# Passages between the layers of a seven-product feed-forward: the sixth product's epilogue first, the seventh's parted, its casts behind a bank copy

## The chip, the cores and the metric

The kernel runs on one core of a Trainium2 chip. The metric is the device time of one execution in microseconds (us); lower is better. Before the change the median of three runs is 3420.51 us (3419.1 to 3424.62). One further execution was taken with the profiler; all rows of the trace come from that one.

The engines are TensorE (PE in the profile; PEld is its load of weights), VectorE (DVE), ScalarE (ACT), GpSimd (POOL) and SyncE (SP, which issues the loads from memory). Each works through its own instructions in order and waits at an instruction until what it needs is there.

## The reference

Two blocks run on 512 tokens of width 1024. The first has a hybrid mixer (gated delta rule and retention) and a feed-forward; the second has two layers, each with a feed-forward, a second mixer and another feed-forward. The change lies in the feed-forward alone, of which there are five:

```
def swiglu(h, w_in, w_out):
    gate, up = jnp.split(h @ w_in, 2, axis=-1)
    return (jax.nn.silu(gate) * up) @ w_out
# first block:  D_FF = 2816, x + g2 * swiglu(modulate(rms_norm(x)))
# second block: D_FF_2 = 2816, layer_norm(ALPHA * x + 0.5 * swiglu(x)), twice in each of 2 layers
```

Everything is in float32. The products run on TensorE as three products of halves: every operand is cast to a rounded high part and a rest, and high·high + high·rest + rest·high is summed.

## The kernel before, in words

**Quads and seven products.** In a feed-forward, `run_quads` takes most of the matrix work. A `Quad` is a 2 by 2 arrangement of weight blocks that meets a 2 by 2 arrangement of activations (`Left`, with the slots A11, A12, A22 and the sums S1 to S4). Instead of eight block products it needs seven, called `mm(e,j)` with j from 1 to 7. Each takes 6·nk matmuls of 128x256, where nk is 4 for quads of the first layer (w1, reading the tile `xa`) and 3 or 2 for quads of the second (w2, reading the tile `hl`, the hidden values). A product accumulates in PSUM: products 1 and 2 in a tile `pj`, product 4 in another, products 3, 5, 6 and 7 in one of three banks `sd`.

**Epilogues.** After product j stands `after(e,j)`: after 1 ScalarE copies the PSUM tile to a bank (`L177`), after 3 and 5 it copies banks on (`L179`, `L181`), after 2, 5, 6 and 7 the use of the quad follows. For a quad of the first layer the use is `gated`: after 6 (`c12`) VectorE forms half of the hidden block h (L257, L259), and `c12b` splits it into the slots A11 and A12 of `hl` (ScalarE's cast L80, VectorE's rest L81). After 7 (`c21`) ScalarE takes the Silu (L264) and VectorE forms the other half (L265); `c21b` and `c21c` form the sums (L113 to L120) and split S2, A22 and S3 into `hl`.

**Weights.** Each product's weights are cast by ScalarE (L164, `cast`) and the rest is formed by VectorE (L166, `rest`); sums of weight blocks are VectorE's L161. The products are cast two positions ahead; three places for cast weights go round (two pairs `whi`/`wlo` and one inside the tile `xa`).

**Groups and passages.** The eleven hidden blocks of a feed-forward are worked in the groups (0,3), (3,3), (6,2), (8,3), the first two blocks by plain products. In each of the first three groups the quads of w1 are followed by two quads of w2, called O1 and O2 here, which read what the group has just written to `hl`. The last w1 quad of the group is called L. So there are three passages to a feed-forward, from L to O1 and O2, and 15 in all. The order of products there is (L,2) ... (L,6), (L,7), (O1,1), (O2,1), (O1,2), (O1,3) ... (O1,6), (O1,7), (O2,2) and so on; then the next w1 quad N begins. O1 and O2 have nk = 3 in the first two groups and nk = 2 in the third. (O1,1) reads A11 and (O1,2) reads A12 of `hl`; (O1,3) reads S2; (O1,7) reads A22. (O1,2) accumulates onto (O1,1) in the same PSUM tile, so it must come after the copy L177 has read that tile.

**Order of the work.** `run_quads` writes the order out by hand for PE, ACT, DVE and SP. At position s it first issues the loads, then the matmuls of product s, then the epilogue of product s-1, the sums of weights, one waiting step of other quads (`step`), and the cast and rest of product s+2. At a passage, while `late` holds, the sums and the cast and rest come ahead of the epilogue: in the kernel before, `late` holds for products 6 and 7 of L. L has a use of its own, `at_once`, which does everything after product 7 in one step.

Of the kernel before, what the change touches and what calls it, by code (L numbers as in the profile page):

```python
# [73 lines left out]
def tmp(e,n=512,name="t"):  # L74
    return e.tp.tile([P,512],F32,tag="t",name=name,bufs=e.tb)

def pair(t): return t.rearrange("p (a b) -> p a b",a=2)
# [112 lines left out]
def run_quads(e, quads, extra):  # L190

    ET=mybir.EngineType
    seq=[]; left=None; done=set()
    for i,q in enumerate(quads):
        if q.needs and left: seq.append((left,7)); left=None
        if q not in done: seq.append((q,1))
        if q.needs: seq.append((quads[i+1],1)); done.add(quads[i+1])
        if left: seq.append((left,7))  # L200
        seq+=[(q,j) for j in (2,3,4,5,6)]; left=q
    seq.append((left,7))
    pos={(id(q),j):s for s,(q,j) in enumerate(seq)}
    at={}; free=-99
    for q in quads:
        g=lambda j: pos[id(q),j]
        for s,t in ((g(1)-6,0),(g(3)-9,5),(g(2)-8,6),(max(g(3)-6,free),3),(g(3)-4,1),(g(3)-3,2),(g(5),4)): at.setdefault(s,[]).append((q,t))
        free=g(5)-1
    with e.tc.manual_schedule(engines={ET.PE,ET.Activation,ET.DVE,ET.SP}):
        for s in range(min(at),len(seq)+1):  # L210
            for q,t in at.get(s,[]):
                if t in (0,5,6): q.load(e,t)
            put=None; keep=None
            if s>0: put=seq[s-1]
            if 0<=s<len(seq):
                q,j=seq[s]
                for d in q.needs:
                    if j==1: d.all(6)
                    if j==3: d.all(7)
                if j==2 and put==(q,1): q.after(e,1); put=None  # L220
                q.mm(e,j)
                if j==7 and s+1<len(seq) and seq[s+1][1]==2: keep=seq[s+1][0]
            nx=seq[s+2] if 0<=s+2<len(seq) else None
            late=put and put[1] in (6,7) and any(put[0] is q.needs[-1] for q in quads if q.needs)
            def weights():
                for q,t in at.get(s,[]):
                    if t in (1,2,3,4): q.sum(e,t)
                if nx and late: nx[0].cast(e,nx[1]); nx[0].rest(e,nx[1])
            if late: weights()
            if put and not (put[1]==1 and put[0] in done): put[0].after(e,put[1])  # L230
            if not late: weights()
            for q in quads:
                for j in (2,5,6,7):
                    if s>0 and (q,j)!=put: q.step(j)
            if keep in done: keep.after(e,1)
            for f in extra.get(s,[]): f()
            if nx and not late: nx[0].cast(e,nx[1]); nx[0].rest(e,nx[1])
        for q in quads:
            for j in (2,5,6,7): q.all(j)
# [3 lines left out]
def htile(e): return e.fp.tile([P,4,256],F32,tag="h",name="h",bufs=3)  # L243
# [7 lines left out]
def gated(e, H, i, hscale, sums, last):  # L251

    nc=e.nc; u=Use()
    def c11(ps):
        u.g=e.ea.tile([P,512],F32,tag="ea",name="g0",bufs=2); nc.scalar.activation(u.g,ps,AF.Silu)
    def c12(ps,E):
        t=tmp(e); nc.vector.tensor_add(t,ps,E)  # L257
        u.h=htile(e)
        nc.vector.scalar_tensor_tensor(u.h[:,0:2,:],pair(u.g),hscale,pair(t),op0=ALU.mult,op1=ALU.mult)  # L259
    def c12b(ps,E): H.first(e,i,u.h[:,0:2,:])  # L260
    def c22(ps,E):
        u.t=tmp(e); nc.vector.tensor_sub(u.t,E,ps)
    def c21(ps):
        g=tmp(e); nc.scalar.activation(g,ps,AF.Silu)  # L264
        nc.vector.scalar_tensor_tensor(u.h[:,2:4,:],pair(g),hscale,pair(u.t),op0=ALU.mult,op1=ALU.mult)  # L265
    v=nc.vector
    def part(p): u.s=H.sums(e,i,u.h[:,0:2,:],u.h[:,2:4,:],p,v,p and u.s); return u.s
    def c21b(ps):
        if sums: u.p0=part(0); u.p1=part(1)
        if last: H.puts(e,i,0,u.p0)  # L270
        H.second(e,i,u.h[:,2:4,:])
        if last: H.puts(e,i,1,u.p1)
    def c21c(ps):
        if sums and not last: H.puts(e,i,0,u.p0); H.puts(e,i,1,u.p1)
    u.c11,u.c12,u.c22,u.c21=[c11],[c12,c12b],[c22],[c21,c21b,c21c]
    if last:
        def at_once(ps): c21(ps); c21b(ps)
        u.c21=[at_once]
    return u

GAB=4
# [3 lines left out]
def ffn(e, w1, w2, acc, hscale, ln):  # L285

    nc=e.nc
    with ExitStack() as cf:
# [30 lines left out]
        for g,(j0,n) in enumerate(GROUPS):  # L319
            last=g==len(GROUPS)-1  # L320
            G=[Quad(e.XA,w1[j],4,gated(e,HP if last else H,j-j0,hscale,not last,not last and j==j0+n-1)) for j in range(max(j0,PLAIN),j0+n)]; Q+=G
            if not last: Q+=[out_quad(e,H,w2[g][i],n,4*i,lambda m,sl,ps,sgn,new,g=g: acc(g,m,2,sl,pair(ps),sgn,new),() if i else G) for i in range(2)]
            else:
                x={2: [lambda: hsums(PLAIN-1)]}
                run_quads(e,Q,x)
                stage2(e,[w2[g][m//4][m%4] for m in range(8)],2*n,lambda m,sl,ps: acc(g,m,1,sl,ps,1,True),ln,HP)
# [1062 lines left out]
```

## Time and profile before

| what | value |
|---|---|
| median of three runs | 3420.51 us |
| profiled execution, its own time | 3430.6 us |
| its span, first to last instruction | 3428.8 us |
| TensorE busy | 3263.1 us, 95% of the span |
| TensorE weight load busy | 2989.2 us, 87% |
| VectorE busy | 2539.7 us, 74% |
| ScalarE busy | 1709.2 us, 50% |
| mean granted TensorE clock | 0.98 of full speed |

The profiled execution's own time is 1.8 us more than its span and 10.1 us more than the median of the runs. A row of a wait names who waited, for whom, the total, how often, and the longest. A row of the timeline gives the start, the length, engine, line, operation, output and inputs, how many instructions are merged in it, and in brackets how long the engine stood idle before it and who released it. Matmuls follow each other at a shorter distance than the length of one, so the start of the next row tells more than the length.

### The profile page before, as it was taken

How to read it: one execution, taken by the hardware profiler on the slowest of the kernel's cores; microseconds unless marked ns; L12 is line 12 of the kernel's file. 1: busy time of each engine (PE TensorE's matmuls, PEld its weight loads, DVE VectorE, ACT ScalarE, POOL GpSimd, SP SyncE). 2: the span in 40 equal slices, each digit the busy share in tenths (PEclk: the TensorE clock that was granted, in tenths of full speed). 3: DMA queues.
4: the chain of work that ended last, by engine and by line, in shares of the span. 5: the costliest groups of instructions: out<-in, count | busy, mean ns of one | idle time of the engine just before them, and what ended most of it. 6: DMA issues, size and time to landing. Idle time of an engine off the chain costs nothing. (4 is left out here: it accounts for less than half of the span.)

```text
span 3428.8 us, 54643 instructions
## 1 busy us (share of the span) xinstructions
PE 3263.1 (95%) x22011; PEld 2989.2 (87%) x22011; DVE 2539.7 (74%) x4101; ACT 1709.2 (50%) x2640; POOL 199.3 (6%) x237
## 2 busy tenths in 40 slices
PE   6989889899999999999999999999999999999998
PEld 3767778899999999878889999999998788899998
DVE  5858877789968988653447888788976634368987
ACT  4544544455555555672224555545546822245554
POOL 3241221000000000110000000000000100000000
PEclk9999999999999999999999999999999999999999
DMA  6221214222332323333331233322332233322232
GB/s 207 67 70 44 74 57 141 82 97 96 100 114 74 105 99 99 99 93 97 95 116 52 91 102 104 102 71 93 99 107 97 94 97 99 98 83 85 93 105 62
DMA packets 103502, 322.09 MB, mean 94 GB/s; under 512 B 11472, under 2 KB 15184, under 8 KB 103248
## 3 DMA queue, kind: packets, MB, share of 16 engines
q1 hardware_dynamic: 102464, 316.04, 28.8%
q8 instruction: 173, 2.83, 0.3%
q0 software_dynamic: 640, 2.10, 0.2%
q14 instruction: 81, 0.66, 0.1%
q10 hardware_dynamic: 144, 0.45, 0.0%
HBM read 316.45 MB, written 2.10 MB: 93 GB/s over the span
## 5 line engine op out<-in xcount | busy, mean ns | idle before, releaser
L43 ACT CAST xa<-wraw 128x1024 fp32r<-128x1024 f32 (+1 forms) x200 | 202.4, 1016 | 385.2 <-PE pj L71 150.0
L166 DVE TENSOR_TENSOR wlo<-wraw,whi 128x1024 fp32r<-128x1024 f32 (+2 forms) x295 | 316.3, 1074 | 48.3 <-ACT whi L164 46.1
L70 PE MATMUL pj<-xa 128*128 128x512 f32 (+1 forms) x968 | 343.1, 355 | 1.4 <-ACT X L966 1.4
L72 PE MATMUL pj<-xa 128*128 128x512 f32 (+1 forms) x968 | 341.9, 354 | 0.0
L71 PE MATMUL pj<-xa 128*128 128x512 f32 (+1 forms) x968 | 341.3, 353 | 0.0
L44 DVE TENSOR_TENSOR xa<-wraw,xa 128x1024 fp32r<-128x1024 f32 (+1 forms) x190 | 224.5, 1184 | 110.0 <-ACT xa L43 108.1
L164 ACT CAST whi<-wraw 128x1024 fp32r<-128x1024 f32 (+2 forms) x295 | 272.3, 926 | 61.5 <-DVE wraw L161 26.2
L129 PE MATMUL sd<-xa,whi 128*128 128x256 f32 x1760 | 229.1, 283 | 0.0
L129 PEld LDWEIGHTS sd<-xa,whi 128*128 128x128 f32 x1760 | 219.1, 192 | 0.0
L129 PE MATMUL sd<-xa 128*128 128x256 f32 x1680 | 213.0, 283 | 0.0
L129 PEld LDWEIGHTS sd<-xa 128*128 128x128 f32 x1680 | 206.6, 192 | 0.0
L70 PEld LDWEIGHTS pj<-xa 128*128 128x128 f32 x968 | 187.1, 193 | 21.9 <-ACT X L966 1.8
L71 PE MATMUL sd<-xa 128*128 128x512 f32 (+1 forms) x600 | 204.7, 341 | 0.0
L70 PE MATMUL sd<-xa 128*128 128x512 f32 (+1 forms) x600 | 203.8, 341 | 0.9 <-DVE X L1230 0.9
L129 PE MATMUL pj<-xa,whi 128*128 128x256 f32 x1520 | 200.0, 285 | 4.2 <-ACT sd L177 4.2
L71 PEld LDWEIGHTS pj<-xa 128*128 128x128 f32 x968 | 187.2, 193 | 19.2
L72 PE MATMUL sd<-xa 128*128 128x512 f32 (+1 forms) x600 | 203.8, 340 | 0.0
L72 PEld LDWEIGHTS pj<-xa 128*128 128x128 f32 x968 | 186.9, 193 | 18.7
L129 PEld LDWEIGHTS pj<-xa,whi 128*128 128x128 f32 x1520 | 190.9, 193 | 5.9 <-ACT sd L177 5.5
L44 DVE TENSOR_TENSOR wlo<-wraw,whi 128x1024 fp32r<-128x1024 f32 (+1 forms) x88 | 109.1, 1241 | 97.6 <-ACT whi L43 97.1
L166 DVE TENSOR_TENSOR xa<-wraw,xa 128x1024 fp32r<-128x1024 f32 (+2 forms) x155 | 169.5, 1094 | 16.0 <-ACT xa L164 14.4
L43 ACT CAST whi<-wraw 128x1024 fp32r<-128x1024 f32 (+1 forms) x88 | 90.1, 1025 | 183.1 <-issue 93.2
(560 smaller groups left out, 8235.2 us busy)
## 6 DMA issues: line engine op xcount, KB each, us to landing
wraw<-in_f_dram SPq DMA_DIRECT2D x176, 512.0 KB, 4.0
wraw<-in_win_dram SPq DMA_DIRECT2D x144, 512.0 KB, 3.5
wraw<-in_f_dram SPq DMA_DIRECT2D x96, 384.0 KB, 3.2
wraw<-in_ff_dram SPq DMA_DIRECT2D x44, 512.0 KB, 4.0
raw<-in_ada_dram SPq DMA_DIRECT2D x48, 256.0 KB, 2.6
wraw<-in_ff_dram SPq DMA_DIRECT2D x24, 384.0 KB, 3.2
wraw<-in_ada_dram SPq DMA_DIRECT2D x16, 512.0 KB, 3.9
wraw<-in_f_dram SPq DMA_DIRECT2D x32, 256.0 KB, 2.8
```

The lines of the kernel that those rows point to most:

```text
L43: nc.scalar.copy(hi[:,:n],raw[:,:n])
L44: (nc.gpsimd if e.wi%e.gp==0 else nc.vector).tensor_sub(lo[:,:n],raw[:,:n],hi[:,:n].bitcast(F32))
L70: nc.tensor.matmul(o,lhsT=hi[:,c],rhs=ah,start=start and k==k0,stop=False)
L71: nc.tensor.matmul(o,lhsT=hi[:,c],rhs=al,start=False,stop=False)
L72: nc.tensor.matmul(o,lhsT=lo[:,c],rhs=ah,start=False,stop=stop and k==nk-1)
L129: nc.tensor.matmul(ps[:,p*256:p*256+256],lhsT=w[:,j:j+128],rhs=A.t[:,c,k,l,:],start=first,stop=last,skip_group_check=True)
L164: s.w[j]=hilo_tile(e); e.nc.scalar.copy(s.w[j][0][:,:s.n],s.raw(j)[:,:s.n])
L166: hi,lo=s.w[j]; n=s.n; e.nc.vector.tensor_sub(lo[:,:n],s.raw(j)[:,:n],hi[:,:n].bitcast(F32))
```

## The change

Three things change in `run_quads` and `gated`, all at the 15 passages. `late` holds for product 7 of L only: after product 6 the epilogue `c12` comes ahead of the sum of weights and of the cast and rest of (O2,1), and the split of A11 and A12 (`all(6)`) follows in the same step, ahead of that cast too. L's epilogue after product 7 is parted: `c21s` takes the Silu, the second half of h and the sums, and `c21p` does the three splits. `c21p` is called one position later, by `all(7)`, behind `after(O1,1)`, which is the copy L177 of O1's first bank.

```
-            late=put and put[1] in (6,7) and any(put[0] is q.needs[-1] for q in quads if q.needs)
+            late=put and put[1]==7 and any(put[0] is q.needs[-1] for q in quads if q.needs)
...
             if late: weights()
             if put and not (put[1]==1 and put[0] in done): put[0].after(e,put[1])
             if not late: weights()
+            if s+1<len(seq) and seq[s+1][0].needs and seq[s+1][1]==1: put[0].all(6)
+            if s>1 and seq[s-1][0].needs and seq[s-1][1]==1: seq[s-1][0].needs[-1].all(7)
...
     def c21b(ps):
         if sums: u.p0=part(0); u.p1=part(1)
-        if last: H.puts(e,i,0,u.p0)
         H.second(e,i,u.h[:,2:4,:])
-        if last: H.puts(e,i,1,u.p1)
     def c21c(ps):
-        if sums and not last: H.puts(e,i,0,u.p0); H.puts(e,i,1,u.p1)
+        if sums: H.puts(e,i,0,u.p0); H.puts(e,i,1,u.p1)
     u.c11,u.c12,u.c22,u.c21=[c11],[c12,c12b],[c22],[c21,c21b,c21c]
     if last:
-        def at_once(ps): c21(ps); c21b(ps)
-        u.c21=[at_once]
+        def c21s(ps): c21(ps); u.p0=part(0); u.p1=part(1)
+        def c21p(ps): H.puts(e,i,0,u.p0); H.second(e,i,u.h[:,2:4,:]); H.puts(e,i,1,u.p1)
+        u.c21=[c21s,c21p]
```

The instructions are the same in number and kind. On PE, POOL and SP their order is the same as before; on ACT and DVE it differs at the 15 passages. The file has one line more, so in the changed kernel the lines from 231 on are up to two higher (L264 becomes L266, L257 becomes L259), those behind `gated` one.

ScalarE at the first passage of the first feed-forward (nk = 3), before. The first L164 belongs to (O1,1), the one with `xa` to (O2,1), the third to (O1,2) and the last to (O1,3); L80 from `h` 128x2x256 is A11/A12, from `s` S2 and S3, from `h` 128x256 A22; L264 is the Silu after (L,7).

```order
L181 COPY sd_5189<-sd_5190 128x512
L164 CAST whi<-wraw 128x768
L164 CAST xa<-wraw 128x768
L80 CAST hl<-h 128x2x256
L164 CAST whi<-wraw 128x768
L264 ACTIVATE t<-sd_5189 128x512
L80 CAST hl<-s 128x2x256
L80 CAST hl<-h 128x256
L80 CAST hl<-s 128x2x256
L177 COPY sd_5190<-pj 128x512
L164 CAST whi<-wraw 128x768
```

And with the change, the same stretch of ScalarE:

```order
L181 COPY sd_5189<-sd_5190 128x512
L164 CAST whi<-wraw 128x768
L80 CAST hl<-h 128x2x256
L164 CAST xa<-wraw 128x768
L164 CAST whi<-wraw 128x768
L266 ACTIVATE t<-sd_5189 128x512
L177 COPY sd_5190<-pj 128x512
L80 CAST hl<-s 128x2x256
L80 CAST hl<-h 128x256
L80 CAST hl<-s 128x2x256
L164 CAST whi<-wraw 128x768
```

The cast of A11/A12 went up past the cast of (O2,1), and the copy L177 went up past the three casts of S2, A22 and S3.

VectorE at the same passage, before. The first L166 is the rest of (O1,1), the one with `xa` that of (O2,1); L257 and L259 are `c12`; L81 is the rest of A11/A12; L161 are sums of O1's weights; L265 is the second half of h.

```order
L166 TENSOR_TENSOR wlo<-wraw,whi 128x768
L161 TENSOR_TENSOR wraw<-wraw 128x768
L166 TENSOR_TENSOR xa<-wraw,xa 128x768
L257 TENSOR_TENSOR t<-sd_5191,t 128x512
L259 SCALAR_TENSOR_TENSOR h<-g_6395,t 128x512
L81 TENSOR_TENSOR hl<-h,hl 128x2x256
L161 TENSOR_TENSOR wraw<-wraw,t_6466 128x768
L166 TENSOR_TENSOR wlo<-wraw,whi 128x768
L265 SCALAR_TENSOR_TENSOR h<-t 128x512
```

And with the change:

```order
L166 TENSOR_TENSOR wlo<-wraw,whi 128x768
L259 TENSOR_TENSOR t<-sd_5191,t 128x512
L261 SCALAR_TENSOR_TENSOR h<-g_6395,t 128x512
L161 TENSOR_TENSOR wraw<-wraw 128x768
L81 TENSOR_TENSOR hl<-h,hl 128x2x256
L166 TENSOR_TENSOR xa<-wraw,xa 128x768
L161 TENSOR_TENSOR wraw<-wraw,t_6466 128x768
L166 TENSOR_TENSOR wlo<-wraw,whi 128x768
L267 SCALAR_TENSOR_TENSOR h<-t 128x512
```

The two instructions of `c12` went up past one sum and one rest, and L81 past that rest; the sum now stands between `c12` and L81. Behind L265 (L267) the order of VectorE is unchanged.

## Rows read from the trace of the kernel before

**Rows 1.** First part of the page: busy us (share), instructions.

```profile
PE 3263.1 (95%) x22011; PEld 2989.2 (87%) x22011; DVE 2539.7 (74%) x4101; ACT 1709.2 (50%) x2640; POOL 199.3 (6%) x237
```

**Rows 2.** TensorE's waits: total us, times, longest.

```profile
PE pj L129 <- ACT sd L177: 33.1, 22, 2.2
...
PE pj L129 <- DVE hl L81: 5.1, 15, 0.3
```

**Rows 3.** Timeline of the first passage, nk = 3: start, us, instruction, [idle before].

```profile
702.11 3.04 PE L129 MATMUL sd<-xa 128*128 128x256 f32 x24
...
705.40 0.95 DVE L161 TENSOR_TENSOR wraw<-wraw 128x768 f32<-128x768 f32 x1
...
707.14 0.69 DVE L257 TENSOR_TENSOR t<-sd,t 128x512 f32<-128x512 f32 x1
...
707.87 1.12 PE L129 MATMUL pj<-hl,whi 128*128 128x256 f32 x8
708.59 0.62 ACT L80 CAST hl<-h 128x512 fp32r<-128x512 f32 x1 [3.72 <-DVE h L259]
...
709.24 0.69 DVE L81 TENSOR_TENSOR hl<-h,hl 128x512 fp32r<-128x512 f32 x1 [0.69 <-ACT hl L80]
...
711.17 2.32 PE L129 MATMUL pj<-hl,xa 128*128 128x256 f32 x18
711.59 0.68 DVE L265 SCALAR_TENSOR_TENSOR h<-t 128x512 f32<-128x512 f32 x1
...
713.23 0.62 ACT L80 CAST hl<-s 128x512 fp32r<-128x512 f32 x1 [2.79 <-DVE s L114]
...
714.58 0.58 ACT L177 COPY sd<-pj 128x512 f32<-128x512 f32 x1
...
715.09 0.82 ACT L164 CAST whi<-wraw 128x768 fp32r<-128x768 f32 x1
...
715.21 1.70 PE L129 MATMUL pj<-hl,whi 128*128 128x256 f32 x12 [1.72 <-ACT sd L177]
...
717.46 1.60 PE L129 MATMUL sd<-hl,whi 128*128 128x256 f32 x12
```

**Rows 4.** Timeline behind the second passage, nk = 3.

```profile
808.99 3.92 PE L129 MATMUL pj<-hl,xa 128*128 128x256 f32 x18 [1.73 <-ACT sd L177]
```

**Rows 5.** Timeline behind the second passage, up to the next w1 quad's second product.

```profile
816.50 0.96 DVE L166 TENSOR_TENSOR wlo<-wraw,whi 128x768 fp32r<-128x768 f32 x1 [0.82 <-ACT whi L164]
...
837.14 1.05 ACT L164 CAST whi<-wraw 128x1024 fp32r<-128x1024 f32 x1 [3.27 <-DMA wraw<-in_ff_dram]
...
839.37 2.08 PE L129 MATMUL pj<-xa,whi 128*128 128x256 f32 x16
```

**Rows 6.** Timeline of the third passage, nk = 2, and of what follows.

```profile
876.81 0.93 PE L129 MATMUL pj<-hl,whi 128*128 128x256 f32 x5
877.34 0.69 DVE L81 TENSOR_TENSOR hl<-h,hl 128x512 fp32r<-128x512 f32 x1 [0.69 <-ACT hl L80]
...
882.65 0.61 ACT L164 CAST whi<-wraw 128x512 fp32r<-128x512 f32 x1
882.77 1.22 PE L129 MATMUL pj<-hl,whi 128*128 128x256 f32 x8 [2.15 <-ACT sd L177]
...
883.30 0.69 DVE L166 TENSOR_TENSOR wlo<-wraw,whi 128x512 fp32r<-128x512 f32 x1 [0.23 <-ACT whi L164]
...
887.14 0.69 DVE L166 TENSOR_TENSOR wlo<-wraw,whi 128x512 fp32r<-128x512 f32 x1 [0.43 <-ACT whi L164]
...
907.63 1.21 PE L129 MATMUL pj<-xa,wlo 128*128 128x256 f32 x8 [1.14 <-DVE wlo L166]
```

**Rows 7.** Stretches: us, busy per engine, granted clock, DMA share, GB/s.

```profile
806.00:816.00 10.00, 8.27 (x57) 8.06 (x56) 7.74 (x14) 5.10 (x9) 0.00 (x0) 0.83 0.00 0
880.00:890.00 10.00, 7.85 (x66) 7.65 (x65) 9.11 (x18) 6.79 (x13) 0.00 (x0) 1.00 0.23 48
...
3290.00:3300.00 10.00, 7.85 (x53) 7.65 (x52) 7.80 (x16) 5.32 (x10) 0.00 (x0) 0.83 0.11 28
```

## Prediction

> **What bounds the kernel now.** I read the engines' busy shares first, then the waits of TensorE, then the timeline of the passages, then stretches with the granted clock. TensorE is busy 95% of the span and VectorE 74% [rows 1], so time is to be won where TensorE stands still. In its list of waits the one by the copy L177 is large, 33.1 us in 22 waits, and the one by L81 comes exactly 15 times [rows 2]; 15 is the number of passages.
>
> The first passage shows how these waits arise [rows 3]. From 702.11 to 707.87 TensorE does 48 matmuls, so one takes 0.12 us, and a product takes 2.16 us with nk = 3, 1.44 with nk = 2, 2.88 with nk = 4. From (O1,1) at 707.87, three products without a wait would bring (O1,3) at 707.87 + 3 x 2.16 = 714.35. It comes at 717.46: 3.1 us are lost. Of these 711.17 - 707.87 - 2.16 = 1.1 fall in (O1,1), whose last third needs what L80 and L81 split off, and 715.21 - 711.17 - 2.16 = 1.9 between (O2,1) and (O1,2), which may not write where L177 has not yet read. L177 starts at 714.58, though (O1,1) ended by 711.2: it stands behind the cast of S2, which waits for VectorE until 713.23, and two more.
>
> **The change at a passage with nk = 3 (10 of the 15).** Durations are those of rows 3.
>
> Epilogue first: the add of `c12` takes the place of the sum at 705.40; its input is there, since (L,6) ends at 702.11 + 3.04 = 705.15. From the start of the add to that of the cast L80 it was 708.59 - 707.14 = 1.45, so the cast runs from 706.85 to 707.47. The sum (0.95) fills VectorE from about 706.8 to 707.7, and L81 ends at about 708.3. (O1,1) needs the cast at its ninth matmul, 707.87 + 8 x 0.12 = 708.83, and the rest at 708.95. Both are there with 0.6 to spare, so the 1.1 us go. (O1,1) then ends at 710.03 and (O2,1) at 712.19. The sum and the rest of (O2,1) that were passed come 1 to 2 us later; that rest now ends near 709.2 and is needed after twelve matmuls of (O2,1), at 711.5. TensorE's own work hides it, with 2.3 us of cover.
>
> Parted epilogue: VectorE no longer idles 0.69 before L81, the sum fills that. L265 and the four short sums behind it thus come 0.7 earlier, and S2's cast may start at 713.23 - 0.7 = 712.5.
>
> The copy: the last matmul of (O1,1) is done near 710.2, so L177 runs from about 710.3 to 710.9, before (O2,1) ends. The 1.9 us go. The copy is a new wait at the head of ScalarE's queue; behind it stand the casts of S2, A22 and S3 and the cast for (O1,3), and for these wait VectorE's rests and TensorE. It holds nobody up, since S2's source comes only at 712.5, 1.6 after the copy.
>
> What is late next: the weights of (O1,3). From S2's cast to the end of the three casts it was 714.58 - 713.23 = 1.35, so their cast starts at 713.85 and ends (0.82) at 714.7. TensorE is there at 712.19 + 2.16 = 714.35 and waits 0.35, and a product after a wait took 717.46 - 715.21 = 2.25, so 0.1 more. The new loss is 0.45 against 3.1: a gain of 2.65. This new wait isn't in the trace; its bounds are 0 (VectorE a little earlier) and the 1.25 that the next part finds with nk = 2. I take 0.35, from these rows; the ends move the sum by +3.5 and -9 over ten passages.
>
> Does TensorE keep the lead? In the second passage's wake the tightest place is N's second product: its cast, late by a load, ends at 838.19, 1.2 us before TensorE comes at 839.37 [rows 5]. So ScalarE and VectorE must come at least 1.45 earlier as well. VectorE has 0.7 from the passage and can shed its own idle time behind it, of which 0.82 is one wait [rows 5]; the load is let go by a VectorE sum and comes as much earlier. I count the lead as kept: 10 x 2.65 = 26.5 us.
>
> **The passage with nk = 2 (5 of 15).** Without waits (O1,3) would start at 876.81 + 3 x 1.44 = 881.13; it started 1.44 + 0.1 after 882.77, at 884.31, so 3.2 are lost [rows 6]. The sum here is shorter and (L,6) is not done when its turn comes, so I give VectorE 0.4 instead of the 0.69 idle before L81. The cast for (O1,3) stood at 882.65; 0.4 and the copy's 0.5 ahead of it go, and it ends at 882.65 - 0.9 + 0.61 = 882.36. TensorE is there at 881.13 and waits 1.25: it is 1.9 nearer. But here VectorE is the bound: it is busy 9.11 of 10 us [rows 7], and at 907.63 TensorE waits 1.14 for one of its rests [rows 6]. No work is taken from VectorE, so TensorE gains in the end what VectorE stops idling: 0.4 + 0.23 + 0.43 = 1.1 [rows 6]. 5 x 1.1 = 5.5 us; the ends are 0 and 5 x 1.9 = 9.5.
>
> The Trainium skill says in Perfetto Trace Analysis, Identifying the Most-Contended Engine, that what counts is improving the engine with the highest occupancy, and that for TensorE the weight load is to be read instead of the matmul rows. In the stretch 880 to 890 that is VectorE (9.11 against 7.65), and the trace agrees there. By that rule taken everywhere, the ten other passages would be capped like these five, which is the second rival below.
>
> **The clock.** After the stall of the second passage the product of 18 matmuls took 3.92 us [rows 4] against 2.32 [rows 3]: 1.6 us more, while the granted clock of that stretch is 0.83, that is, a third of it ran at 1.2 GHz instead of 2.4. So it was in six of the 15 passages, the first and the last of which are in rows 7; after the wait of 1.14 us at 907.63 it did not happen. With the waits down to 0.45 and 1.3 us I expect none of the six. Three are passages with nk = 2, where VectorE decides and part of the loss is hidden, so I take 1.4 each: 8.4 us, between 0 (first rival) and 9.6.
>
> The Trainium skill, TensorE: Matmul & The Clock Gate, Why this matters for your kernels, warns only of longer pauses than any of these passages has. By that rule the six falls would have another cause and stay, and 8.4 us would be missing from the sum. The rows speak against it: the fall begins right behind the stall.
>
> **Sum.** 26.5 + 5.5 + 8.4 = 40.4 us. PE, POOL and SP keep their order, and between passages TensorE goes on as before, so nothing else moves. Against the profiled execution's own 3430.6 us that gives 3390.2. This execution lies 10.1 above the median of the runs; the waits are of the program, so I take the same 40.4 off the median: 3420.5 - 40.4 = 3380.
>
> **Rivals.**
> 1. The clock falls stay, behind the short new waits or wherever they happen to lie. For: where a fall lies differs between passages of one kind. Against: none followed a wait near 1.1 us. Gain 32.0: 3388.5.
> 2. VectorE binds behind all 15 passages, and TensorE waits later for what it has won. For: VectorE is taken to 91% behind a passage with nk = 2 [rows 7], and behind one with nk = 3 N's second product has but 1.2 spare [rows 5]. Against: that place did not wait before. Gain 15 x 1.1 = 16.5: 3404.
> 3. The lead is eaten almost wholly by the next load, since loads are let go by what ScalarE and VectorE use up; rows 5 show 3.27 us of ScalarE waiting for one. Against: these loads follow work that comes earlier. Within 0.2% of before, say 3417.
> 4. Slower: the weights of (O2,1). Their cast now stands behind the cast of A11/A12 and their rest behind L81, at about 709.2 with 2.3 to spare. Were that cast late by its load, TensorE would wait at (O2,1); each us beyond 2.3 costs one, and from 2.3 + 2.65 = 5 us on the passage is slower than before. At 6 us it is 1.05 x 15 = 16 us slower: 3436. Against: none of the waits in rows 3 is for a load.
>
> **How the numbers follow.** Forecast 62%, its own range 3374 to 3387 (the ends of the new wait, of the nk = 2 part and of the clock, not all at once); rival 1 14%, rival 2 15%, rival 3 6%, rival 4 3%. The 80% range goes from 3373 to 3403: all of the forecast and of rival 1, and the better half of rival 2. About 0.2% (7 us) is what a measurement tells from no change; by that, the first three cases are faster (91%), rival 3 is the same (6%), rival 4 slower (3%).
>
> **What would show it.** In the profile after: TensorE's wait by L177 down from 33.1 us to under 5, since only copies outside the passages are left; the waits by L81 gone from 15 passages; a new wait of TensorE for the cast L164 at (O1,3), 0.3 to 0.5 us in ten passages and 1.0 to 1.4 in five; waits for VectorE's rest behind the nk = 2 passages longer than 1.14; stretches behind the passages at a clock of 1.00. It is wrong if TensorE waits longer than 1.3 at (O1,3), if rests of VectorE stop TensorE behind nk = 3 passages (rival 2), if 0.83 still stands there (rival 1), or if (O2,1) waits for its weights (rival 4).

## The result and the profile after

The changed kernel takes 3385.28 us (median of four runs, 3382.02 to 3386.9), the kernel before 3422.57 us beside it on the same chip (3419.1 to 3427.46). The ratio is 0.9887 with a 95% interval of 0.9875 to 0.9898, so 35 to 43 us less, 37 by the medians. A second series of the same two kernels gave 0.9891 (0.9877 to 0.9906). The forecast was 3380, with 3374 to 3387 as its own range.

First the page after, to be read against [rows 1]: every engine has as many instructions as before, and TensorE needs 16 us less for the same 22011 matmuls. The profiled execution took 3385.98 us, with a span of 3384.1.

```profile
PE 3246.9 (96%) x22011; PEld 2975.3 (88%) x22011; DVE 2535.4 (75%) x4101; ACT 1706.0 (50%) x2640; POOL 199.7 (6%) x237
```

TensorE's waits after (total us, times, longest), against [rows 2]:

```profile
PE pj L129 <- DVE wlo L166: 8.8, 5, 6.0
PE sd L129 <- ACT whi L164: 7.0, 15, 1.0
...
PE pj L129 <- ACT sd L177: 5.0, 7, 0.9
```

L177 has come down from 33.1 us in 22 waits to 5.0 in 7; the seven lie outside the moved place. The sign named for it was a wait under 5; 5.0 stands at its edge. L81 has no row any more. A row that was not there has come: 15 waits for the cast L164, the weights of (O1,3). The first row is the same as before, 8.8 us in 5 waits.

The first passage of the kernel after, in its timeline (start, us, instruction, idle before), against [rows 3]:

```profile
706.26 0.95 DVE L161 TENSOR_TENSOR wraw<-wraw 128x768 f32<-128x768 f32 x1
706.38 0.62 ACT L80 CAST hl<-h 128x512 fp32r<-128x512 f32 x1 [2.84 <-DVE h L261]
707.13 0.69 DVE L81 TENSOR_TENSOR hl<-h,hl 128x512 fp32r<-128x512 f32 x1
707.40 1.60 PE L129 MATMUL pj<-hl,whi 128*128 128x256 f32 x12
...
709.76 0.57 ACT L177 COPY sd<-pj 128x512 f32<-128x512 f32 x1 [0.79 <-PE pj L129]
...
711.72 1.60 PE L129 MATMUL pj<-hl,whi 128*128 128x256 f32 x12
712.02 0.62 ACT L80 CAST hl<-s 128x512 fp32r<-128x512 f32 x1 [1.70 <-DVE s L114]
713.38 0.83 ACT L164 CAST whi<-wraw 128x768 fp32r<-128x768 f32 x1
714.26 1.70 PE L129 MATMUL sd<-hl,whi 128*128 128x256 f32 x12 [0.23 <-ACT whi L164]
```

(O1,1) starts at 707.40, and its operands are there: the cast ended at 707.00, and L81, with no idle ahead of it, at 707.82. (O1,2) follows at 711.72, which is 4.32 or two products later, so nothing is lost up to there. The copy runs at 709.76, as soon as (O1,1) has ended, and ScalarE then waits 1.70 for the source of S2, so the copy delays nobody. (O1,3) comes at 707.40 + 6.86 instead of + 6.48: 0.38 lost, where 3.1 were lost before.

Stretches behind passages in the kernel after (columns as in [rows 7]), two with nk = 3, then two with nk = 2:

```profile
793.00:813.00 20.00, 19.83 (x165) 19.63 (x165) 19.45 (x29) 11.72 (x19) 0.00 (x0) 1.00 0.21 64
1151.00:1171.00 20.00, 19.82 (x165) 19.62 (x164) 19.79 (x29) 12.63 (x20) 0.00 (x0) 1.00 0.30 99
868.00:888.00 20.00, 18.40 (x145) 17.39 (x145) 19.64 (x39) 12.52 (x23) 0.00 (x0) 1.00 0.25 93
3246.00:3256.00 10.00, 8.98 (x75) 8.78 (x75) 9.88 (x19) 6.50 (x13) 0.00 (x0) 1.00 0.11 27
```

The granted clock is 1.00, where [rows 7] have 0.83. Behind nk = 3 TensorE is busy 99% in both stretches; behind nk = 2 it is 92 and 90%. VectorE is busy 97 and 99% behind nk = 3 and 98 and 99% behind nk = 2, so its share in such a stretch does not tell the two kinds of passage apart. What TensorE waits for does: the five waits for VectorE's rest L166 in the list above are the 6.0, which lies outside the passages, and four behind nk = 2 (1.12 and three of 0.56); behind nk = 3 there is none.

To compare whole kernels I take one sum from every trace: the time that TensorE loses at the 15 passages against 0.12 us per matmul, from the start of (O1,1) to the twentieth product after it, which lies in the quads behind. Before it is 64.6 us, after 21.2. That makes 43.4, and it splits like this. The seven passages with nk = 3 that have no clock fall lose about 2.63 less each, which is 26.3 for ten. The two with nk = 2 that have none lose 1.35 and 1.55 less, which is 7.2 for five at their mean. The other 9.9 is the remainder, in the passages with the six falls. In the quads outside these stretches TensorE loses 18.4 before and 18.4 after, and 18.0 to 18.7 in every profile of this document, so nothing moved there.

### The profile page after: what moved, and what is told of

Read it like the earlier page. It is cut to its first block, busy times and chain, and to the rows that moved or that the text cites. A ratio compares the mean times of both kernels' runs of the same rounds, so it can differ in the third digit from the quotient of the medians.

```text
span 3384.1 us, 54643 instructions
## 1 busy us (share of the span) xinstructions
PE 3246.9 (96%) x22011; PEld 2975.3 (88%) x22011; DVE 2535.4 (75%) x4101; ACT 1706.0 (50%) x2640; POOL 199.7 (6%) x237
## 4 chain that ended last, share of the span: by engine, by line
PE 46%; DVE 5%; ACT 3%; issue 2%; DMA 0%; POOL 0%; ACTq 0%; DVEq 0%; POOLq 0%; SPq 0%
PE sd L129 10%; PE pj L129 8%; PE pj L71 5%; PE pj L70 5%; PE pj L72 5%; PE sd L71 4%; PE sd L72 4%; PE sd L70 4%; DVE wraw L161 1%; DVE wlo L166 1%; PE ps L368 1%; DMA wraw<-in_f_dram 0%; DVE X L617 0%; PE ps L373 0%; DVE hl L81 0%
## 5 line engine op out<-in xcount | busy, mean ns | idle before, releaser
L166 DVE TENSOR_TENSOR wlo<-wraw,whi 128x1024 fp32r<-128x1024 f32 (+2 forms) x295 | 315.6, 1071 | 25.5 <-ACT whi L164 23.2
L164 ACT CAST whi<-wraw 128x1024 fp32r<-128x1024 f32 (+2 forms) x295 | 272.4, 927 | 58.9 <-DVE wraw L161 28.7
L166 DVE TENSOR_TENSOR xa<-wraw,xa 128x1024 fp32r<-128x1024 f32 (+2 forms) x155 | 169.2, 1092 | 15.2 <-ACT xa L164 13.3
```

The lines of the kernel that those rows point to most:

```text
L164: s.w[j]=hilo_tile(e); e.nc.scalar.copy(s.w[j][0][:,:s.n],s.raw(j)[:,:s.n])
L166: hi,lo=s.w[j]; n=s.n; e.nc.vector.tensor_sub(lo[:,:n],s.raw(j)[:,:n],hi[:,:n].bitcast(F32))
```

## The experiments

The runs in one table; each has its own runs of the kernel before beside it (medians 3425.75 in the first series, 3421.15 in the second). "Lost" is the sum just described. The changed kernel did not run in the first series, to which the first four edits belong, and the kernel before alone differs by 1 to 5 us between series; so from one edit to another the lost sum tells more than the medians.

| kernel | median us (lowest to highest) | ratio to before, 95% | lost, us |
|---|---|---|---|
| before (first profile, two more) | 3422.57; 3425.75; 3421.15 | 1 | 64.6; 64.0, 67.0 |
| after | 3385.28 (3382.02 to 3386.9) | 0.9875 to 0.9898 | 21.2 |
| after, again | 3383.44 (3383.0 to 3386.78) | 0.9877 to 0.9906 | 21.4 |
| first epilogue alone | 3412.84 (3409.17 to 3417.85) | 0.9945 to 0.9972 | 49.9 |
| parting alone | 3393.93 (3391.93 to 3394.89) | 0.9888 to 0.9919 | 31.3 |
| fewer additions | 3377.65 (3372.65 to 3379.67) | 0.9839 to 0.9867 | 14.2 |
| cast ahead | 3379.9 (3378.19 to 3390.32) | 0.9850 to 0.9885 | 20.0 |
| cast ahead, GpSimd | 3387.62 (3385.86 to 3390.45) | 0.9888 to 0.9921 | 25.9 |

**The first epilogue alone.** The changed kernel with the parting taken back:

```diff
-            if s>1 and seq[s-1][0].needs and seq[s-1][1]==1: seq[s-1][0].needs[-1].all(7)
...
-        u.c21=[c21s,c21p]
+        def at_once(ps): c21(ps); c21b(ps)
+        u.c21=[at_once]
```

> Only the first half of the change: c12 and the split of A11/A12 come ahead of the sum and of the cast and rest of (O2,1); the epilogue of the seventh product stays in one step and the copy L177 behind its three casts. My theory: the wait inside (O1,1) goes (1.1 us at nk = 3), but the copy comes only 0.7 us earlier, so TensorE waits for it longer, 2.3 us instead of 1.9. Gain 0.7 in ten passages and 0.4 in five, 9 us; half-clock stretches behind passages stay (four to eight of 15). Rival (the waits by L81 and by L177 are independent and add): 1.1 in ten and 0.8 in five, 15 us. Rival (the half clock has nothing to do with these stalls): no half clock behind passages, or as often as with the whole change.

Measured: 12.9 us less than before. (O1,1) loses nothing any more (1.1 before), but (O1,2) now waits longer for the copy. TensorE's waits and the first passage in this kernel:

```profile
PE pj L129 <- ACT sd L177: 38.4, 22, 2.4
```

```profile
703.66 1.60 PE L129 MATMUL pj<-hl,whi 128*128 128x256 f32 x12
...
708.28 0.62 ACT L80 CAST hl<-s 128x512 fp32r<-128x512 f32 x1 [3.06 <-DVE s L114]
...
709.63 0.58 ACT L177 COPY sd<-pj 128x512 f32<-128x512 f32 x1
...
710.26 1.70 PE L129 MATMUL pj<-hl,whi 128*128 128x256 f32 x12 [2.11 <-ACT sd L177]
```

TensorE arrives earlier and stands before the same queue: the copy is still behind the casts of S2, A22 and S3, and its place in time did not move as far as TensorE's. From the start of (O1,1) the copy now comes at 5.97 instead of 6.71, 0.74 earlier, while TensorE comes 1.1 earlier. Lost are 2.24 to 2.28 there with nk = 3 (1.88 before) and 2.58 with nk = 2 (2.31 before). So the two waits do not simply add, and that rival is out by these rows, though the time alone (12.9, with 9 expected and 15 for the rival) could not tell. Three clock falls are in this profile, where four to eight were expected.

**The parting alone.** The changed kernel with `late` as before and the line for `all(6)` taken out:

```diff
-            late=put and put[1]==7 and any(put[0] is q.needs[-1] for q in quads if q.needs)
+            late=put and put[1] in (6,7) and any(put[0] is q.needs[-1] for q in quads if q.needs)
-            if s+1<len(seq) and seq[s+1][0].needs and seq[s+1][1]==1: put[0].all(6)
```

> Only the second half: the epilogue of the seventh product is parted and its three casts follow the copy L177; c12 stays behind the sum and the cast and rest of (O2,1). My theory: the 1.1 us in (O1,1) stay, the 1.9 before (O1,2) go, and the cast for (O1,3) is there in time at nk = 3 (wait 0 to 0.1) and 0.9 late at nk = 2. Gain 10 x 1.9 + 5 x 0.7 = 22.5 us, and the half-clock stretches behind the passages go (up to 8 us more): 23 to 31 us. Rival (VectorE binds everywhere behind the passages): 15 x 0.7 = 10 us, with TensorE waiting for rests behind nk = 3.

Measured: 31.8 us less, a little above the 23 to 31 expected. TensorE's waits in this kernel:

```profile
PE pj L129 <- DVE hl L81: 5.1, 15, 0.3
PE pj L129 <- ACT sd L177: 5.0, 7, 0.9
...
PE sd L129 <- ACT whi L164: 3.7, 5, 0.8
```

The copy's waits are down to the seven, those by L81 stay at 15, and the new wait at (O1,3) comes in the five passages with nk = 2 only: with 1.1 lost in (O1,1), TensorE reaches (O1,3) too late to wait there with nk = 3. No clock fall is left at a passage. No wait for a rest has come behind nk = 3, so the rival is out. Of the two halves this is the larger. In lost time they win 14.7 and 33.3, together 4.6 more than the whole change's 43.4: this half takes all six falls away and the other half three, which are counted twice. At passages without a fall the halves add up to the whole: 0.7 + 1.9 for 2.6 with nk = 3, 0.5 + 1.0 for 1.55 with nk = 2.

**Fewer additions.** Is VectorE the bound behind nk = 2? The changed kernel without 4 of the 12 additions to X of each such passage's second-layer quads; that part of the result is missing.

```diff
+    if nk==2: u.c12=u.c12[:1]; u.c22=u.c22[:1]
```

> The changed kernel, but the two second-layer quads with nk = 2 leave out four of their twelve additions to the residual X on VectorE (the ones that read the copy E of the fourth product), so this part of the result is missing. It takes about 2.4 us of VectorE off behind each nk = 2 passage (3.2 in the first feed-forward) and changes neither loads nor ScalarE casts. My theory (VectorE binds there): TensorE's lost time between (O1,3) and the next w1 quad, 1.5 to 3.4 us per passage with the change, falls to 0.1 to 1.0; 6 to 10 us less than the changed kernel. Rival (loads or ScalarE's casts bind there): those losses stay, 0 to 1 us less.

Measured: the loss behind (O1,3) falls from 3.42, 1.54, 2.53, 1.54 and 1.55 to 1.05, 0.18, 2.28, 0.19 and 0.18 us, 6.7 in all, and the median lies 6 to 8 under the two of the changed kernel. In TensorE's waits two of the five for VectorE's rest L166 remain:

```profile
PE pj L129 <- DVE wlo L166: 6.2, 2, 6.0
```

So VectorE is the bound there, in four of the five passages. In the third feed-forward's only 0.25 came of it; there casts of weights wait 1.53 and 2.93 us for loads in the kernel after, and TensorE waits at both places for the copy L177, which stands behind the cast:

```profile
2063.04 0.62 ACT L164 CAST whi<-wraw 128x512 fp32r<-128x512 f32 x1 [1.53 <-DMA wraw<-in_f_dram]
...
2064.19 1.21 PE L129 MATMUL pj<-hl,whi 128*128 128x256 f32 x8 [0.95 <-ACT sd L177]
...
2075.28 1.05 ACT L164 CAST whi<-wraw 128x1024 fp32r<-128x1024 f32 x1 [2.93 <-DMA wraw<-in_f_dram]
...
2076.87 2.18 PE L129 MATMUL pj<-xa,whi 128*128 128x256 f32 x16 [0.72 <-ACT sd L177]
```

**The cast ahead.** The changed kernel with the cast for (O1,3) directly behind the copy and ahead of the three splits; its rest stays behind them.

```diff
-            if s>1 and seq[s-1][0].needs and seq[s-1][1]==1: seq[s-1][0].needs[-1].all(7)
+            ahead=s>1 and seq[s-1][0].needs and seq[s-1][1]==1
+            if ahead: nx[0].cast(e,nx[1]); seq[s-1][0].needs[-1].all(7)
...
-            if nx and not late: nx[0].cast(e,nx[1]); nx[0].rest(e,nx[1])
+            if nx and not late:
+                if not ahead: nx[0].cast(e,nx[1])
+                nx[0].rest(e,nx[1])
```

> The changed kernel with ScalarE's cast for (O1,3) moved ahead of the casts of S2, A22 and S3, directly behind the copy L177; VectorE's rest stays behind the three splits. My theory: TensorE's new wait for that cast goes: 0.35 + 0.1 us in ten passages, 4.5 us; at nk = 2 the 1.2 us go at (O1,3) but come back as waits for VectorE, so nothing is won there. 4 to 5 us less than the changed kernel. Rival (S2, not the weights, is what comes last at (O1,3)): the wait stays, now for the cast or rest of S2, and the time is the same or up to 5 us longer. Rival (nk = 2 is not bound by VectorE): 10 us less.

Measured: 3379.9, 3.5 to 5.4 us under the two medians of the changed kernel, but the intervals overlap; in lost time it is 1.3 less. The wait at (O1,3) is gone in all 15. With nk = 3 nine of ten passages lose 0.00 to 0.60; with nk = 2 all five lose what they lost (4.60, 2.73, 3.63, 2.73, 2.74 against 4.60, 2.72, 3.71, 2.72, 2.73), now while TensorE waits for VectorE's rests:

```profile
PE pj L129 <- DVE wlo L166: 8.7, 5, 5.9
PE pj L129 <- ACT sd L177: 7.0, 8, 2.0
...
PE sd L129 <- DVE wlo L166: 4.6, 5, 0.9
```

A wait of 1.0 was taken away and nothing was won: this is the sign of a bound elsewhere. This run alone cannot tell a VectorE that has no time left from a rest that merely stands late in its order, behind the three splits; the run before, in which less of VectorE's work brought TensorE forward, names the first for what follows (O1,3). No run has both edits. The one other passage with nk = 3 lost 2.26 to a load:

```profile
3090.33 2.21 SPq L37 DMA_DIRECT2D wraw<-in_f_dram  x4
...
3095.50 0.83 ACT L164 CAST whi<-wraw 128x768 fp32r<-128x768 f32 x1 [3.83 <-DMA wraw<-in_f_dram]
3096.24 0.58 ACT L177 COPY sd<-pj 128x512 f32<-128x512 f32 x1
```

The cast waits 3.83 us for data, and the copy of the next bank stands behind it.

**GpSimd for some additions.** The kernel just described, with four additions of each nk = 2 passage moved to GpSimd in four of the five feed-forwards:

```diff
-            else: nc.vector.tensor_tensor(x,x,ps,op=op)
+            else: (nc.vector if new or g!=2 else nc.gpsimd).tensor_tensor(x,x,ps,op=op)
```

> e4_cast_ahead, and in the four feed-forwards of the second block the four additions per nk = 2 passage that read the copy E from SBUF go to GpSimd, so that VectorE has 2.4 us less there and nothing is left out. My theory (VectorE binds behind nk = 2): TensorE's lost time there falls from 2.7 to 0.2 to 1.0 us in the feed-forwards that no load binds, 4 to 8 us less than e4_cast_ahead. Rival (GpSimd, slower per element, holds back VectorE's next addition to the same part of X, or VectorE itself at the memory): lost time stays or grows, 0 to 6 us longer.

Measured: 3387.62, slower than without the edit, so my theory fell and its rival held, in its second form: VectorE never waits for a GpSimd addition to X, but its own operations take longer. The four passages lose 4.71 to 4.73 each, where they lost 2.73, 3.63, 2.73 and 2.74. The second feed-forward's:

```profile
1237.48 0.68 DVE L166 TENSOR_TENSOR wlo<-wraw,whi 128x512 fp32r<-128x512 f32 x1
...
1238.68 1.22 DVE L166 TENSOR_TENSOR xa<-wraw,xa 128x1024 fp32r<-128x1024 f32 x1
...
1240.57 2.21 POOL L620 TENSOR_TENSOR X<-X,t 128x512 f32<-128x512 f32 x1 [6.02 <-DVE X L620]
1241.55 1.78 DVE L166 TENSOR_TENSOR wlo<-wraw,whi 128x512 fp32r<-128x512 f32 x1
...
1244.01 2.21 POOL L620 TENSOR_TENSOR X<-X,t 128x512 f32<-128x512 f32 x1 [1.22 <-DVE X L620]
1244.99 2.31 DVE L166 TENSOR_TENSOR wlo<-wraw,whi 128x1024 fp32r<-128x1024 f32 x1
```

While GpSimd adds, a rest on VectorE takes 1.78 instead of 0.68 and 2.31 instead of 1.22. The first of these ends at 1243.33, 0.55 after GpSimd's addition does (1242.78), so most of its own 0.68 seems to fall behind that. Of the four additions moved away from VectorE at a passage (0.68 each) three lengthen a rest in this way, by 1.1 in all cases but one. Beside the remaining one VectorE adds from PSUM, in the 0.67 or 0.68 that this takes elsewhere too. The Trainium skill, Perfetto Trace Analysis, Optimizing Scalar/DVE Operations, says that GpSimd and VectorE share a read port, so that moving work between them need not help; the trace agrees.

**The clock falls.** Two more profiles of the kernel before:

> The kernel before, unaltered, profiled again. It tells how many of its 15 passages a half-clock stretch follows in another execution. My theory (a fall can follow the stall, it need not): the stalls are the same to 0.1 us and the number of falls another one than six, between two and eight; the span then lies 1.2 to 1.6 us from 3428.8 per fall more or less. Rival (the falls belong to fixed passages): the same six passages.

> The kernel before, unaltered, profiled a third time; as b1_same.

Measured: six and eight falls at passages, after six in the first profile, and not at the same ones; so the rival of fixed passages is out, and the expected "another number than six" came once of twice. The stalls are the same to 0.1 but for two in (O1,1) (1.83, 1.52 and 1.52 in the eleventh passage, 0.83, 0.84 and 1.17 in the sixth). Two stretches of the third: the second passage has its fall (0.91), and the one behind the last passage, at 0.83 in [rows 7], is not there:

```profile
793.00:813.00 20.00, 17.72 (x131) 17.11 (x130) 16.50 (x25) 9.19 (x15) 0.00 (x0) 0.91 0.17 57
3290.00:3300.00 10.00, 8.26 (x69) 8.26 (x70) 8.96 (x17) 7.26 (x14) 0.00 (x0) 1.00 0.32 100
```

In all, 20 of the 45 passages of the kernel before have a stretch at half clock behind the stall, 3 of 15 with the first epilogue alone, and none of 90 in the other six profiles. So the falls go with the stalls. Not with the single stall at the copy, which was longer with the first epilogue alone (2.24 to 2.58, for 1.88 to 2.31) and had fewer; but before it the kernel before loses 0.8 to 1.8 in (O1,1) as well, so that 3.1 and more are lost up to (O1,3), against 2.3 to 2.7 with the first epilogue alone and at most 1.7 in the other six profiles, where a later stall for a load (2.2 lost, with the cast ahead) had no fall either. Whether that sum decides is not shown, and what decides in the single case stays open. That the span goes with the number of falls was not seen: 3428.8, 3417.5 and 3425.1 with six, six and eight. The stages outside the quads differ by more between executions (2036.0, 2025.5, 2030.1 us), and so does the mean granted clock (0.980, 0.984, 0.980); why is not shown.

> The changed kernel once more, unaltered, for a second profiled execution and more timed ones. My theory: TensorE's lost time at each passage comes out the same to 0.1 us (0.36 and 0.34 at nk = 3, 1.18 at nk = 2), and no half-clock stretch lies at a passage. Rival (the clock's falls lie where they happen to lie): one to six passages with a half clock again. Time 37 us, 35 to 41, below the kernel before.

Measured: 3383.44, the same losses as in the first profile of the kernel after (21.4 in sum for 21.2), and again no fall at a passage.

## Why the prediction was right

**The wait in (O1,1).** Right: the cast ended 0.4 ahead of (O1,1), as walked (707.47 against 707.87), and 1.1 are gone in each passage with nk = 3. The first epilogue alone shows that 0.7 of the 1.1 is kept while the copy stays late.

**The copy.** Right: 710.3 was walked, and measured from the start of (O1,1) it came 0.07 earlier. The parting alone shows that this half carries most of the change.

**The new wait.** Right in size: 0.32 to 0.38 lost before (O1,3) with nk = 3 and 0.1 in it, where 0.35 + 0.1 was taken, and 1.18 with nk = 2 for 1.25. The cast of S2 came at 4.62 after (O1,1) for 4.63. The move of VectorE by 0.7 that carries this is thus shown.

**The lead with nk = 3.** Right: only 0.09 to 0.26 is lost up to the twentieth product. The second rival (VectorE binds behind all 15) and the third (the loads eat the gain) are out, and so is the fourth: (O2,1) loses nothing. The term of 26.5 measured 26.3.

**The term of nk = 2.** The mechanism was right and the size low: 1.35 and 1.55 at the two passages without a fall for 1.1, so 7.2 for 5.5. The step that failed is "I give VectorE 0.4 instead of the 0.69 idle before L81". It rested on (L,6) not being done when the add's turn came. In the third passage of the kernel after, VectorE has no idle before any of these:

```profile
867.78 0.69 DVE L261 SCALAR_TENSOR_TENSOR h<-g,t 128x512 f32<-128x512 f32 x1
...
868.39 0.68 DVE L161 TENSOR_TENSOR wraw<-wraw 128x512 f32<-128x512 f32 x1
...
869.16 0.69 DVE L81 TENSOR_TENSOR hl<-h,hl 128x512 fp32r<-128x512 f32 x1
```

The timeline marks none up to 892 us either, so all three idles of [rows 6] went whole, 0.69 + 0.23 + 0.43 = 1.35, and that is what was won. The fourth feed-forward's passage agrees: its idles before were 0.69 + 0.23 + 0.62 = 1.54, and 1.55 was won.

```profile
2450.80 0.69 DVE L81 TENSOR_TENSOR hl<-h,hl 128x512 fp32r<-128x512 f32 x1 [0.69 <-ACT hl L80]
...
2456.76 0.69 DVE L166 TENSOR_TENSOR wlo<-wraw,whi 128x512 fp32r<-128x512 f32 x1 [0.23 <-ACT whi L164]
...
2460.60 0.69 DVE L166 TENSOR_TENSOR wlo<-wraw,whi 128x512 fp32r<-128x512 f32 x1 [0.62 <-ACT whi L164]
```

The sign that I named, waits for rests longer than 1.14, did not come: the longest there is 1.12. The bound shows in the idle time that went, and in the run that took work from VectorE, not in a longer single wait, and not in the busy share alone, which is as high behind nk = 3. The Trainium skill's rule of the engine with the highest occupancy (Perfetto Trace Analysis, Identifying the Most-Contended Engine), read by stage, fits behind nk = 2, where VectorE has 9.88 of 10 us and the weight load 8.78. Behind nk = 3 it does not help: from 1151 to 1171 VectorE has 19.79 of 20 and the weight load 19.62, and yet TensorE lost only 0.43 at that passage; the measurement decides.

**The clock.** Right in kind: the first rival is out, since none of the falls stayed. The term of 8.4 is near: the remainder is 9.9 in that profile, and 0.7 of it is no fall but the eleventh passage's longer wait in (O1,1) (1.83 for 1.1), where VectorE's rest, and the epilogue behind it, came late after a cast that waited 2.14 for a load:

```profile
2372.64 0.84 ACT L164 CAST whi<-wraw 128x768 fp32r<-128x768 f32 x1 [2.14 <-DMA wraw<-in_f_dram]
```

A fall costs about 1.5 with nk = 3 (4.55 against 3.1 lost) and 1.3 at the last passage (5.58 against 4.25 in the profile where it has none). The Trainium skill (TensorE: Matmul & The Clock Gate, Why this matters for your kernels) warns only of longer pauses; these runs show the falls coming and going with single stalls of at most 2.6 us, and the measurement decides.

**The sum.** 26.3 + 7.2 + 9.9 = 43.4 for 40.4. The spans of the two first profiles differ by 44.7: 43.4 at the passages and 1.3 outside the quads (2036.0 and 2034.7 us). So the three terms explain the profiles. The medians differ by 37 only. The profiled execution of the kernel before was 8.0 above the median of these runs, that of the kernel after 0.7, and I took a sum read in a slow execution off the median. The stages outside the quads alone differ by 10.6 between three executions of the kernel before; what kept some 6 of the 43 out of the medians is not shown. That 3380 came within 5 of the result is so in part luck: the terms were 3 too small, and the medians gave 6 less than the passages.

## What to carry to other kernels

Look at what stands ahead of a PSUM-freeing copy in its engine's queue: here three casts that wait for another engine held the copy back, for which TensorE waited 1.9 to 2.3 us at every passage, and letting it pass them was most of the gain. Making only the matmuls ahead of such a copy finish earlier gives part of that back: of 1.1 us, 0.4 came back as a longer wait for the copy. Before paying for the wait that is left, see in that stage whether another engine could keep up: behind nk = 2, where VectorE had no idle time and TensorE already waited for its rests, a wait of 1.0 us taken from TensorE gave nothing. A high share alone does not tell, as VectorE's 97 to 99% behind nk = 3 shows; taking work from the engine in a run does.

## What was not expected of the hardware

A stall of 0.8 to 1.8 us and, one product later, one of 1.9 to 2.3 us were followed by a stretch at half clock in 20 of 45 passages of one and the same program, at other passages in each execution; 0.83 over 10 us [rows 7] makes that stretch 3.4 us long. And GpSimd's addition of 128x512 (2.21 us) more than doubled the rest of 128x512 that VectorE formed beside it, 0.68 to 1.78 us, while an addition of VectorE's that read PSUM kept its 0.68.
